# Rotating 96 images: 16 rows per partition and vector-engine block transposes in place of 4 rows per partition and matmul transposes

## The chip, the cores and the metric

The kernel runs on one core of one Trainium2 chip. The metric is device time in microseconds (us); lower is better. A "span" is the length of one profiled execution, from the first to the last instruction; the timed runs come out about 1.8 us above it.

Engine names: PE is the matmul engine, ACT the scalar engine, DVE the vector engine, SP the engine that here does nothing but issue transfers. The transfers themselves run on the core's 16 DMA engines, which the page counts together; SP issues all loads here and ACT all stores, so there are two DMA queues, q1 (loads) and q10 (stores).

## The reference

```python
x = np.random.randn(32, 3, 256, 256).astype(np.float32)

def reference(x):
    return np.rot90(x, k=1, axes=(-2, -1)).astype(np.float32)
```

These are 96 images of 256 x 256 floats, 25.17 MB in and 25.17 MB out. Each is rotated by a quarter turn: a transpose and a reversal of one axis. There is no arithmetic, so the least that any kernel must do is to move 50.33 MB between memory and the chip.

## The kernel before

A partition holds 4 rows of an image. Four rows of 256 floats are 4 KB that lie together in memory, so each transfer is made of runs of 4 KB. PE transposes 128 x 128 blocks into PSUM (the on-chip memory that PE writes here), ACT casts them to bf16, a second matmul puts the rows in the right order, and DVE copies the result to the output tile.

```python
    x_v4 = x.rearrange("b c (p d) w -> (b c) p d w", d=4)      # 4 rows per partition
    out_v4 = out.rearrange("b c (p d) w -> (b c) p d w", d=4)
    GROUPS = [8] * 11 + [4, 2, 2]                              # images per group
    # ... pools: 4 input tiles, 3 output tiles, 3 tail tiles, 2 + 2 PSUM tiles ...
    for gi, G in enumerate(GROUPS):
        S4 = in_pool.tile([P, G2, 4, W], fp32, tag="S", name="S4")
        nc.sync.dma_start(
            out=S4[:],
            in_=x_v4[i0 : i0 + G].rearrange("(j q) p d w -> (q p) j d w", q=2),
        )
        # ... U4: output tile ...
        for j in range(G2):
            for d4 in range(4):
                for par in range(2):
                    nc.tensor.transpose(...)                   # PE, 8 per image pair
            for q in range(2):
                nc.scalar.copy(out=bt[:], in_=p1pair[:, :, q, :])        # ACT, f32 to bf16
            for hh in range(2):
                for q in range(2):
                    nc.tensor.matmul(out=psum2[...], lhsT=exchh[hh][:], rhs=bts[q][:], ...)
            for hh in range(2):
                nc.vector.tensor_copy(out=U4[:, j, 2 * hh : 2 * hh + 2, :], in_=psum2[:, hh])
        nc.scalar.dma_start(                                   # the last three groups: after the loop
            out=out_v4[i0 : i0 + G].rearrange("(j q) p d w -> (q p) j d w", q=2),
            in_=U4[:],
        )
```

Of the kernel before, what the change touches and what calls it, by code (L numbers as in the profile page):

```python
# [1 line left out]

# [5 lines left out]


@with_exitstack
def kernel(
    ctx: ExitStack,
    tc: tile.TileContext,
    x: bass.AP,
    out: bass.AP,
):
    nc = tc.nc
    B, C, H, W = x.shape
    assert H == W == 256  # L20
    P = 128
    N = B * C

    x_v4 = x.rearrange("b c (p d) w -> (b c) p d w", d=4)
    out_v4 = out.rearrange("b c (p d) w -> (b c) p d w", d=4)

    GROUPS = [8] * 11 + [4, 2, 2]
    assert sum(GROUPS) == N
    assert all(g % 2 == 0 for g in GROUPS)

    fp32 = mybir.dt.float32
    bf16 = mybir.dt.bfloat16

    const_pool = ctx.enter_context(tc.tile_pool(name="const", bufs=1))
    in_pool = ctx.enter_context(tc.tile_pool(name="in_pool", bufs=4))
    bt_pool = ctx.enter_context(tc.tile_pool(name="bt_pool", bufs=4))
    out_pool = ctx.enter_context(tc.tile_pool(name="out_pool", bufs=3))
    tail_pool = ctx.enter_context(tc.tile_pool(name="tail", bufs=1))
    psum1_pool = ctx.enter_context(tc.tile_pool(name="psum1", bufs=2, space=bass.MemoryType.PSUM))
    psum2_pool = ctx.enter_context(tc.tile_pool(name="psum2", bufs=2, space=bass.MemoryType.PSUM))  # L40

    identity = const_pool.tile([P, P], fp32)
    make_identity(nc, identity)

    exchh = []
    for hh in range(2):
        e = const_pool.tile([P, P // 2], bf16, name=f"exch{hh}")
        nc.gpsimd.memset(e, 0.0)  # L48
        nc.gpsimd.affine_select(  # L49
            out=e,  # L50
            in_=e,
            compare_op=mybir.AluOpType.not_equal,
            fill=1.0,
            base=-(P - 1) + hh,
            pattern=[[2, P // 2]],
            channel_multiplier=1,
        )
        exchh.append(e)

    TAIL_N = 3  # L60
    deferred_stores = []

    i0 = 0
    for gi, G in enumerate(GROUPS):
        is_tail = gi >= len(GROUPS) - TAIL_N
        G2 = G // 2
        S4 = in_pool.tile([P, G2, 4, W], fp32, tag="S", name="S4")
        nc.sync.dma_start(
            out=S4[:],
            in_=x_v4[i0 : i0 + G].rearrange("(j q) p d w -> (q p) j d w", q=2),  # L70
        )
        S4_r = S4.rearrange("pp j d (k par) -> pp j d k par", par=2)

        if is_tail:
            U4 = tail_pool.tile(
                [P, G2, 4, W], fp32, tag=f"tail{gi}", name=f"U4_tail{gi}"
            )
        else:
            U4 = out_pool.tile([P, G2, 4, W], fp32, tag="U", name="U4")

        for j in range(G2):
            p1pair = psum1_pool.tile([P, 2, 2, W], fp32, name="p1pair")
            p1pair_r = p1pair.rearrange(
                "k dd q (pt dquad) -> k dd q pt dquad", dquad=4
            )
            for d4 in range(4):
                for par in range(2):
                    nc.tensor.transpose(  # L88
                        p1pair_r[:, 1 - par, :, :, d4],
                        S4_r[:, j, d4, :, par],  # L90
                        identity,
                    )
            bts = []
            for q in range(2):
                bt = bt_pool.tile([P, 2, W], bf16, name="bt")
                nc.scalar.copy(out=bt[:], in_=p1pair[:, :, q, :])  # L96
                bts.append(bt)

            psum2 = psum2_pool.tile([P, 2, 2, W], fp32, name="psum2")
            for hh in range(2):  # L100
                for q in range(2):
                    nc.tensor.matmul(  # L102
                        out=psum2[64 * q : 64 * q + 64, hh],
                        lhsT=exchh[hh][:],
                        rhs=bts[q][:],
                        start=True,
                        stop=True,
                    )

            for hh in range(2):  # L110
                nc.vector.tensor_copy(  # L111
                    out=U4[:, j, 2 * hh : 2 * hh + 2, :], in_=psum2[:, hh]
                )

        if is_tail:
            deferred_stores.append((i0, G, U4))
        else:
            nc.scalar.dma_start(
                out=out_v4[i0 : i0 + G].rearrange("(j q) p d w -> (q p) j d w", q=2),
                in_=U4[:],  # L120
            )
        i0 += G

    for s0, G, U4 in deferred_stores:
        nc.scalar.dma_start(  # L125
            out=out_v4[s0 : s0 + G].rearrange("(j q) p d w -> (q p) j d w", q=2),
            in_=U4[:],
        )


# [1 line left out]
_INS = ['x']  # L132
_OUTS = [((32, 3, 256, 256), 'float32')]


# [23 lines left out]
```

## Time and profile before

| | before |
|---|---|
| time when the prediction was made, median of 3 | 127.58 us (127.54 to 128.63) |
| profiled span | 125.8 us |
| busy: PE, DVE, ACT | 81%, 48%, 41% |
| transfer rate, 40 to 80 us | 420 GB/s |
| data packets | 12,288 of 4 KB (two queues of 6,144) |

The first lines are from the page of the kernel before. The first of them gives each engine's busy us, share of the span and number of instructions. The rows named DMA and GB/s divide the span into 40 equal slices: a 9 means that the 16 DMA engines were busy 90% of the slice or more, and GB/s is what they moved. The queue lines give packets, MB, and the time of those packets as a share of 16 engines' span. The last line is a group of like instructions: source line, engine, operation, output and input with their shapes, count, then busy us, mean ns of one, and the idle time before them with what ended most of it.

```profile
PE 101.3 (81%) x576; PEld 63.0 (50%) x576; DVE 60.5 (48%) x96; ACT 51.9 (41%) x97; POOL 1.2 (1%) x10
...
DMA  3999999999999999999999999999999999999993
GB/s 69 400 409 413 419 409 408 413 397 415 421 421 422 422 418 422 417 418 421 423 419 422 422 419 418 419 421 418 423 422 421 419 415 421 422 404 411 410 413 133
DMA packets 12742, 50.42 MB, mean 401 GB/s; under 512 B 448, under 2 KB 448, under 8 KB 12736
...
q1 hardware_dynamic: 6368, 25.17, 49.7%
q10 hardware_dynamic: 6368, 25.17, 48.9%
...
L111 DVE COPY U<-psum 128x512 f32<-128x512 f32 x88 | 55.5, 684 | 56.7 <-PE psum L102 44.7
```

The two queues together fill 98.6% of the DMA engines' time. DVE's copy of 128x512 floats takes 684 ns. The next view, windows, shows whether the rate follows PE. Its columns are: stretch, its length, busy time and number of instructions of PE, PEld, DVE, ACT and POOL, granted PE clock, DMA share, GB/s.

```profile
40.00:60.00 20.00, 19.67 (x115) 11.88 (x115) 12.24 (x21) 10.45 (x20) 0.00 (x0) 1.00 1.02 420
60.00:80.00 20.00, 16.20 (x99) 10.13 (x98) 9.78 (x17) 8.40 (x16) 0.00 (x0) 1.00 1.02 420
```

PE falls from 19.67 to 16.20 us of 20, and the rate stays at 420 GB/s. PE is busy, but it is not what bounds the kernel. The same is seen in the chain of waits (start, length, what), where the longest pieces are stores:

```profile
47.37 19.88 DMA out_dram<-U
...
73.94 23.12 DMA out_dram<-U
```

### The profile page before, as it was taken

To read this page: it belongs to the slowest core of one execution; us is meant where nothing else is said; L and a number is where in the kernel's file an instruction comes from. 1 tells how busy PE (TensorE), PEld (TensorE's weight loads), DVE (VectorE), ACT (ScalarE), POOL (GpSimd) and SP (SyncE) were. 2 spreads that over 40 slices of the span, in tenths; PEclk is the share of its full clock that TensorE was granted. 3 is DMA by queue.
4 is the path that set the end of the run, shared out by engine and by line. 5 is a ranking of instruction groups with operands and counts; after the bars stand their busy time and mean duration, and the time that the engine had idled before them with its cause. 6 is when DMAs were issued, how large, how long until landed. Compare 5 with 4: busy or idle time off the path is not lost.

```text
span 125.8 us, 1521 instructions
## 1 busy us (share of the span) xinstructions
PE 101.3 (81%) x576; PEld 63.0 (50%) x576; DVE 60.5 (48%) x96; ACT 51.9 (41%) x97; POOL 1.2 (1%) x10
## 2 busy tenths in 40 slices
PE   0029999999999999999995994897897699999500
PEld 0028556475576555655771761654654555755300
DVE  0000655565647744747445542842841945656520
ACT  4003363633653365336434435246246056336300
POOL 3000000000000000000000000000000000000000
PEclk9999999999999999999999999999999999999995
DMA  3999999999999999999999999999999999999993
GB/s 69 400 409 413 419 409 408 413 397 415 421 421 422 422 418 422 417 418 421 423 419 422 422 419 418 419 421 418 423 422 421 419 415 421 422 404 411 410 413 133
DMA packets 12742, 50.42 MB, mean 401 GB/s; under 512 B 448, under 2 KB 448, under 8 KB 12736
## 3 DMA queue, kind: packets, MB, share of 16 engines
q1 hardware_dynamic: 6368, 25.17, 49.7%
q10 hardware_dynamic: 6368, 25.17, 48.9%
q8 instruction: 4, 0.07, 0.2%
q14 instruction: 2, 0.02, 0.0%
HBM read 25.17 MB, written 25.17 MB: 400 GB/s over the span
## 4 chain that ended last, share of the span: by engine, by line
DMA 40%; PE 40%; DVE 7%; ACT 6%; issue 1%; DVEq 1%; ACTq 0%
DMA out_dram<-U 34%; PE p1pair L88 25%; PE psum L102 15%; DMA S<-in_x_dram 6%; ACT bt L96 6%; DVE U L111 4%; DVE U_tail L111 3%; DVEq L154 0%; ACTq L125 0%; DVEq L111 0%; ACTq L96 0%
## 5 line engine op out<-in xcount | busy, mean ns | idle before, releaser
L111 DVE COPY U<-psum 128x512 f32<-128x512 f32 x88 | 55.5, 684 | 56.7 <-PE psum L102 44.7
L96 ACT CAST bt<-p1pair 128x512 bf16<-128x512 f32 x96 | 50.6, 593 | 65.8 <-PE p1pair L88 65.8
L88 PE MATMUL p1pair<-identity,S 128*128 128x128 f32 x384 | 63.9, 305 | 8.8 <-DMA S<-in_x_dram 8.8
L88 PEld LDWEIGHTS p1pair<-identity,S 128*128 128x128 f32 x384 | 52.0, 209 | 30.2 <-issue 25.2
L102 PE MATMUL psum<-bt,exch 128*64 128x512 bf16 x192 | 45.0, 395 | 8.9 <-DVE U L111 7.0
L102 PEld LDWEIGHTS <-exch 128*64 128x64 bf16 x192 | 11.0, 107 | 25.4 <-DVE U L111 9.5
L111 DVE COPY U_tail<-psum 128x512 f32<-128x512 f32 x8 | 5.1, 685 | 3.1 <-PE psum L102 3.1
L96 ACT ACT_TABLE_LOAD x1 | 1.3, 1283 | 0.7 <-PEq L143 0.7
L49 POOL TENSOR_SCALAR_AFFINE_SELECT exch<-exch 128x64 bf16<-128x64 bf16 x2 | 0.4, 238 | 0.0
masks.py:199 POOL TENSOR_SCALAR_AFFINE_SELECT identity<-identity 128x128 f32<-128x128 f32 x1 | 0.3, 292 | 0.0
L48 POOL MEMSET exch<- 128x64 bf16 x2 | 0.2, 151 | 0.0
masks.py:197 POOL MEMSET identity<- 128x128 f32 x1 | 0.2, 204 | 0.3 <-POOLq L143 0.3
L143 POOL MEMSET const-bfloat16-1.0<- 128x1 bf16 x1 | 0.1, 101 | 0.0
L143 POOL MEMSET const-uint8-127<- 128x1 uint8 x1 | 0.1, 101 | 0.0
L143 POOL MEMSET const-float32-0.0<- 128x1 f32 x1 | 0.1, 98 | 0.2 <-issue 0.2
L143 POOL MEMSET const-float32-1.0<- 128x1 f32 x1 | 0.1, 98 | 0.0
## 6 DMA issues: line engine op xcount, KB each, us to landing
S<-in_x_dram SPq DMA_DIRECT2D x11, 2048.0 KB, 17.6
out_dram<-U ACTq DMA_DIRECT2D x11, 2048.0 KB, 18.4
S<-in_x_dram SPq DMA_DIRECT2D x1, 1024.0 KB, 16.8
S<-in_x_dram SPq DMA_DIRECT2D x2, 512.0 KB, 8.5
out_dram<-U_tail ACTq DMA_DIRECT2D x1, 1024.0 KB, 5.8
out_dram<-U_tail ACTq DMA_DIRECT2D x2, 512.0 KB, 5.1
```

The lines of the kernel that those rows point to most:

```text
L48: nc.gpsimd.memset(e, 0.0)
L49: nc.gpsimd.affine_select(out=e, in_=e, compare_op=mybir.AluOpType.not_equal, fill=1.0, base=-(P - 1) + hh, pattern=[[2, P // 2]], channel ...
L88: nc.tensor.transpose(p1pair_r[:, 1 - par, :, :, d4], S4_r[:, j, d4, :, par], identity,)
L96: nc.scalar.copy(out=bt[:], in_=p1pair[:, :, q, :])
L102: nc.tensor.matmul(out=psum2[64 * q : 64 * q + 64, hh], lhsT=exchh[hh][:], rhs=bts[q][:], start=True, stop=True,)
L111: nc.vector.tensor_copy(out=U4[:, j, 2 * hh : 2 * hh + 2, :], in_=psum2[:, hh])
L143: nc = _bacc.Bacc("TRN2", target_bir_lowering=False, num_devices=1)
```

## The change

Its intent is to make the runs longer on both sides. A partition now holds 16 rows of an image, 16 KB that lie together in memory, both for loads and for stores. An image then takes only 16 partitions. The kernel uses DVE's block transpose on blocks of 32 partitions by 32 elements (`A = 32 // K`), so two images share a block, and a second pair of images takes part on the free side: a group has 16 images (4 blocks of partitions, 2 images in each, 2 on the free side). PE, ACT's casts and PSUM are not used any more. The core of the diff:

```diff
-    x_v4 = x.rearrange("b c (p d) w -> (b c) p d w", d=4)
-    out_v4 = out.rearrange("b c (p d) w -> (b c) p d w", d=4)
-    GROUPS = [8] * 11 + [4, 2, 2]
+    R = 16
+    K = H // R          # 16 partitions per image
+    A = 32 // K         # 2 images per block of 32 partitions
+    G = 4 * A * A       # 16 images per group
+    F = R * W           # 4096 floats, 16 KB
+    x_v = x.rearrange("b c h w -> (b c h w)").rearrange(
+        "(g b a qk f) -> g b qk a f", b=A, a=A, qk=4 * K, f=F
+    )
+    o_v = out.rearrange("b c h w -> (b c h w)").rearrange(
+        "(g b a qk f) -> g a qk b f", b=A, a=A, qk=4 * K, f=F
+    )
     ... (PE transposes, casts, second matmul, copies, tail groups: removed) ...
+    in_pool = ctx.enter_context(tc.tile_pool(name="in_pool", bufs=3))
+    out_pool = ctx.enter_context(tc.tile_pool(name="out_pool", bufs=3))
+    for g in range(N // G):
+        S = in_pool.tile([P, A, F], fp32, name="S")
+        for b in range(A):
+            nc.sync.dma_start(out=S[:, b], in_=x_v[g, b])
+        U = out_pool.tile([P, A, F], fp32, name="U")
+        src = S.rearrange("p b (r k q) -> p q r k b", r=R, q=R)[:, ::-1, :, ::-1]
+        dst = U.rearrange("p a (q k r) -> p q r k a", q=R, r=R)
+        for q in range(R):
+            nc.vector.transpose(dst[:, q], src[:, q])
+        for a in range(A):
+            nc.scalar.dma_start(out=o_v[g, a], in_=U[:, a])
```

There are six groups with 16 transposes each. Neighbouring elements of a transpose's input and output are 64 bytes apart, or 16 KB when the step is from one image of a pair to the other.

More of the change, by code (lines that the diff above doesn't have):

```diff
@@ L5 @@
 import concourse.tile as tile
-from concourse import bass_utils, mybir
-from concourse.masks import make_identity
+from concourse import mybir
 from concourse._compat import with_exitstack
@@ L20 @@
     assert H == W == 256
+    N = B * C
     P = 128
-    N = B * C
-    x_v4 = x.rearrange("b c (p d) w -> (b c) p d w", d=4)
-    out_v4 = out.rearrange("b c (p d) w -> (b c) p d w", d=4)
-    GROUPS = [8] * 11 + [4, 2, 2]
-    assert sum(GROUPS) == N
-    assert all(g % 2 == 0 for g in GROUPS)
-    fp32 = mybir.dt.float32
-    bf16 = mybir.dt.bfloat16
-    const_pool = ctx.enter_context(tc.tile_pool(name="const", bufs=1))
-    in_pool = ctx.enter_context(tc.tile_pool(name="in_pool", bufs=4))
@@ L36 @@
-    bt_pool = ctx.enter_context(tc.tile_pool(name="bt_pool", bufs=4))
-    out_pool = ctx.enter_context(tc.tile_pool(name="out_pool", bufs=3))
-    tail_pool = ctx.enter_context(tc.tile_pool(name="tail", bufs=1))
-    psum1_pool = ctx.enter_context(tc.tile_pool(name="psum1", bufs=2, space=bass.MemoryType.PSUM))
-    psum2_pool = ctx.enter_context(tc.tile_pool(name="psum2", bufs=2, space=bass.MemoryType.PSUM))
-    identity = const_pool.tile([P, P], fp32)
-    make_identity(nc, identity)
-    exchh = []
@@ L46 @@
-    for hh in range(2):
-        e = const_pool.tile([P, P // 2], bf16, name=f"exch{hh}")
-        nc.gpsimd.memset(e, 0.0)
-        nc.gpsimd.affine_select(
-            out=e,
-            in_=e,
-            compare_op=mybir.AluOpType.not_equal,
-            fill=1.0,
-            base=-(P - 1) + hh,
-            pattern=[[2, P // 2]],
-            channel_multiplier=1,
-        )
-        exchh.append(e)
-    TAIL_N = 3
-    deferred_stores = []
-    i0 = 0
-    for gi, G in enumerate(GROUPS):
-        is_tail = gi >= len(GROUPS) - TAIL_N
-        G2 = G // 2
-        S4 = in_pool.tile([P, G2, 4, W], fp32, tag="S", name="S4")
-        nc.sync.dma_start(
-            out=S4[:],
-            in_=x_v4[i0 : i0 + G].rearrange("(j q) p d w -> (q p) j d w", q=2),
-        )
-        S4_r = S4.rearrange("pp j d (k par) -> pp j d k par", par=2)
-        if is_tail:
-            U4 = tail_pool.tile(
-                [P, G2, 4, W], fp32, tag=f"tail{gi}", name=f"U4_tail{gi}"
-            )
-        else:
-            U4 = out_pool.tile([P, G2, 4, W], fp32, tag="U", name="U4")
-        for j in range(G2):
-            p1pair = psum1_pool.tile([P, 2, 2, W], fp32, name="p1pair")
-            p1pair_r = p1pair.rearrange(
-                "k dd q (pt dquad) -> k dd q pt dquad", dquad=4
-            )
-            for d4 in range(4):
-                for par in range(2):
-                    nc.tensor.transpose(
-                        p1pair_r[:, 1 - par, :, :, d4],
-                        S4_r[:, j, d4, :, par],
-                        identity,
-                    )
-            bts = []
-            for q in range(2):
-                bt = bt_pool.tile([P, 2, W], bf16, name="bt")
-                nc.scalar.copy(out=bt[:], in_=p1pair[:, :, q, :])
-                bts.append(bt)
-            psum2 = psum2_pool.tile([P, 2, 2, W], fp32, name="psum2")
-            for hh in range(2):
-                for q in range(2):
-                    nc.tensor.matmul(
-                        out=psum2[64 * q : 64 * q + 64, hh],
-                        lhsT=exchh[hh][:],
-                        rhs=bts[q][:],
-                        start=True,
-                        stop=True,
-                    )
-            for hh in range(2):
-                nc.vector.tensor_copy(
-                    out=U4[:, j, 2 * hh : 2 * hh + 2, :], in_=psum2[:, hh]
-                )
-        if is_tail:
-            deferred_stores.append((i0, G, U4))
-        else:
-            nc.scalar.dma_start(
-                out=out_v4[i0 : i0 + G].rearrange("(j q) p d w -> (q p) j d w", q=2),
-                in_=U4[:],
-            )
-        i0 += G
@@ L124 @@
-    for s0, G, U4 in deferred_stores:
-        nc.scalar.dma_start(
-            out=out_v4[s0 : s0 + G].rearrange("(j q) p d w -> (q p) j d w", q=2),
-            in_=U4[:],
-        )
+    R = 16
[3 more added lines that the diff above has]
+    F = R * W
+    fp32 = mybir.dt.float32
+    x_v = x.rearrange("b c h w -> (b c h w)").rearrange(
[4 more added lines that the diff above has]
+    )
```

## The prediction

> **What bounds the kernel now.** The DMA engines. The page's DMA row is at 9 in 38 of 40 slices, and the two hardware queues take 49.7% and 48.9% of 16 engines' span. PE looks busy (81%), but the windows from 30 to 110 us show 420 GB/s whether PE is busy 98% or 83% of a stretch. The chain of waits names PE for 40% because buffers come free through it; its largest pieces are stores of 19.9 and 23.1 us that DVE waits for. About 2.6 us at the start and 2.1 us at the end of the 125.8 us span move almost nothing; the 121 us between run at 416 GB/s: 400 to 414 with loads alone (until 22 us), 420 mixed, 410 with stores alone. The measured 127.58 is 1.8 us above the profiled span.
>
> **What the change does.** It removes PE (101 us busy), ACT's casts (51 us) and 96 DVE copies of 684 ns (60 us), and adds 96 DVE block transposes of 128x512 f32. Bytes stay the same, so nothing removed lies on the critical path. What can move the time:
>
> 1. *Runs of 16 KB instead of 4 KB.* Each 4 KB packet occupied its engine for 157 ns (49.7% of 16 x 125.8 us over 6368 packets), 26.1 GB/s. [...]about 118 us for the data instead of 121: a gain of 2 to 3.5 us. If the hardware cuts at 4 KB the gain is nearly nil.
> 2. *Coarser pipeline.* First stores need 4 MB loaded plus 16 transposes: about 24 us (before: 21.9). Meanwhile three input buffers (12 MB, 30 us of DMA) keep the engines loaded. At the end the last 4 MB must be transposed before they are stored; the previous group's store covers that.
> 3. *DVE.* [...]a transpose takes about 0.68 us (estimate: as the 128x512 copy, 681 ns), 11 us per group of 16 images against 20 us of DMA (8.4 MB at 420 GB/s), 65 us in all: hidden. By my arithmetic DVE stays hidden up to about 1.0 us each. But each element is 64 bytes or 16 KB from the next, on both sides[...]. [...]No trace here shows a strided DVE access. I give that 22%.
>
> **Prediction.** 124.3 us: 4.7 us of ends, 118 us of data, 1.8 us from profile to timing. Range, lopsided for the DVE risk: 121.5 to 139. Faster by over 2% 0.50, within 2% 0.28, slower by over 2% 0.22.
>
> **What would show it.** Step 1: near 3,200 packets instead of 12,742, mixed windows at 425 or more. Step 2: DMA row at 9 in all inner slices, first store near 24 us. Step 3: transposes of 0.65 to 0.75 us, DVE busy near 65 us, waiting mostly for loads or free buffers. If wrong: transposes of 1.1 us or more, DVE busy 85% or more, and a tail in which DVE works while DMA is idle.
>
> **What would make it wrong.** The strided DVE rate; packets cut at 4 KB; memory-side conflicts of the 16 KB runs; a gap between last load and last store.

The sum was put down as 124.3 us; its three terms (4.7, 118 and 1.8) make 124.5. The 118 us of data (427 GB/s over 50.33 MB) stands as the author's estimate, not shown by a trace. In point 3 the 22% and the upper end of the range stand for a kernel bound by DVE, at about 142 us (e6 measured such a case at 140.33).

## The result, and the profile after

| | before | after |
|---|---|---|
| time, median of 4 runs each | 128.06 us (127.54 to 128.63) | 124.50 us (124.27 to 124.52) |
| ratio, 95% interval | | 0.972 (0.968 to 0.976) |
| profiled span | 125.8 us | 122.7 us |
| transfer rate, 40 to 60 us | 420 GB/s | 431 GB/s |
| time of one data packet, median | 159 ns (4 KB) | 611 ns (16 KB) |
| DVE busy | 60.5 us | 90.7 us |

A ratio is the mean time of one kernel's runs over that of the other's runs of the same rounds, so it is not quite the ratio of the medians that are quoted. The change is faster by 2.8%. The outputs are right.

The lines of the page after that answer to those of before:

```profile
DVE 90.7 (74%) x96; POOL 0.2 (0%) x4
...
DVE  0000699999999999999999999999906999930000
...
DMA  3999999999999999999999999999999999999992
GB/s 85 406 433 443 427 427 427 427 427 427 310 432 432 433 433 427 427 433 432 419 433 438 427 427 427 432 438 432 432 427 438 438 427 433 433 427 427 427 432 101
DMA packets 3457, 50.34 MB, mean 410 GB/s; under 512 B 384, under 2 KB 384, under 8 KB 384
...
q1 hardware_dynamic: 1728, 25.17, 48.9%
q10 hardware_dynamic: 1728, 25.17, 47.9%
...
L49 DVE STREAM_TRANSPOSE U<-S 128x512 f32<-128x512 f32 x96 | 90.7, 1055 | 17.7 <-DMA S<-in_x_dram 13.3
```

There are 3,072 data packets of 16 KB in place of 12,288 of 4 KB (the rest, 384 packets under 512 B and one more, is not data). The DMA row is full as before: the same engines are as busy, and each slice moves more. In the windows (the columns are now stretch, length, DVE, POOL, clock, DMA share, GB/s) the rate is 431 and 432 where it was 420:

```profile
40.00:60.00 20.00, 20.00 (x22) 0.00 (x0) 1.00 1.01 431
60.00:80.00 20.00, 19.82 (x22) 0.00 (x0) 1.00 1.01 432
```

Two things are not as expected. A transpose takes 1.06 us by its record, and 0.95 us from one start to the next (90.7 us over 96), not about 0.68. And the GB/s row has one slice at 310, near 32 us, that the kernel before does not have; it is called the dip below. The DMA row stays at 9 there: a packet that takes longer counts as busy too (25 load packets between 30 and 34 us take over 700 ns in place of 611), so a full DMA row is not yet a full rate.

### The profile page after: what moved, and what is told of

Read it like the earlier page. It is cut to its first block, busy times and chain, and to the rows that moved or that the text cites. A ratio compares the mean times of both kernels' runs of the same rounds, so it can differ in the third digit from the quotient of the medians.

```text
span 122.7 us, 182 instructions
## 1 busy us (share of the span) xinstructions
DVE 90.7 (74%) x96; POOL 0.2 (0%) x4
## 2 busy tenths in 40 slices
DMA packets 3457, 50.34 MB, mean 410 GB/s; under 512 B 384, under 2 KB 384, under 8 KB 384
## 4 chain that ended last, share of the span: by engine, by line
DMA 53%; DVE 31%; SPq 1%; issue 1%; DVEq 1%; ACTq 0%
DVE U L49 31%; DMA out_dram<-U 28%; DMA S<-in_x_dram 26%; SPq L43 1%; DVEq L77 1%; ACTq L51 0%; DVEq L49 0%
## 5 line engine op out<-in xcount | busy, mean ns | idle before, releaser
L49 DVE STREAM_TRANSPOSE U<-S 128x512 f32<-128x512 f32 x96 | 90.7, 1055 | 17.7 <-DMA S<-in_x_dram 13.3
```

What stands on the lines that cost most here:

```text
L49: nc.vector.transpose(dst[:, q], src[:, q])
```

## The experiments

Theory 1 is that the gain is the longer packet alone: a packet has a fixed time that does not grow with its size, and four times fewer packets pay it. The rival, theory 2, is that the gain comes from the rest: PE, ACT and PSUM emptied, fewer and larger tiles, a simpler pipeline.

### e1: the changed kernel again, beside e2 to e4 on the same chip

> Control on this chip: the changed kernel unedited. Both theories: 124.3 to 124.7 us, span 122.5 to 122.9, ratio to before 0.972, 16 KB packets of about 611 ns, transposes of 1.05 us, and the dip to about 310 GB/s in the slice near 32 us if it belongs to the kernel and not to one execution.

Measured: 124.78 us (124.35 to 124.88), just above the expected range, ratio 0.974 (0.970 to 0.979), before 127.93 us (127.50 to 128.35) on this chip. The dip is there again, at 288 GB/s in the same slice, so it belongs to the kernel:

```profile
GB/s 85 368 432 442 442 432 432 426 432 426 288 410 426 432 426 432 432 432 448 418 432 442 437 426 426 432 426 432 432 426 432 432 426 432 432 442 426 432 442 107
```

### e2: the kernel before with 16 KB runs

```diff
-            out=S4[:],
-            in_=x_v4[i0 : i0 + G].rearrange("(j q) p d w -> (q p) j d w", q=2),
+            out=S4.rearrange("p j d w -> p (j d w)"),
+            in_=flat(x_f, i0, G),     # the group's images as one stretch, cut in 128 equal runs
     ... the stores alike; all compute unchanged; the result is wrong on purpose ...
```

> The kernel before with nothing changed but the transfers' addresses: 16 KB runs in place of 4 KB (wrong result on purpose); PE, ACT and DVE work and all buffers stay. Theory 1 (packet size): about 3,600 packets of 611 ns, mixed windows at 430 GB/s, span 122.3 to 123.3, time 124.5 to 125.2. Theory 2 (the gain comes from the work taken off PE and ACT or from the larger tiles): time stays at 127.5 to 128.5 although packets are larger.

Measured: 125.27 us (125.22 to 125.45), ratio 0.979 (0.976 to 0.983), span 123.7 us: time and span are just above what theory 1 expected. By the 2% rule the verdict is "unclear", but the interval lies well under 1. The rate with PE at 19.64 of 20 us (columns as in the windows of before):

```profile
40.00:60.00 20.00, 19.64 (x115) 11.92 (x115) 12.24 (x20) 10.46 (x20) 0.00 (x0) 1.00 1.01 431
```

What follows: the addresses of the transfers alone, with all of the old compute in place, bring 2.66 us (127.93 less 125.27). The expected packet count was 3,600 and the page has 4,039 in all, because the small last groups keep runs of 8 KB and 4 KB. That is of use, since one run then holds three sizes: the median packet took 159 ns for 4 KB, 309 ns for 8 KB and 611 ns for 16 KB. From 4 to 16 KB that is 452 ns for 12,288 bytes, 27.2 GB/s per engine, and what is left of each packet is about 8 ns (159 less 4,096 bytes at 27.2 GB/s). The records of packets overlap a little, though: the DMA share is 1.02 with 4 KB and 1.01 with 16 KB. Worked out from the rates instead, 16 engines at 420 and 431 GB/s spend 156.0 ns on 4 KB and 608.2 ns on 16 KB, which leaves about 5 ns fixed (an estimate, and the one that counts for the time).

### e3: the changed kernel with 4 KB runs

```diff
-            nc.sync.dma_start(out=S[:, b], in_=x_v[g, b])
+            nc.sync.dma_start(
+                out=S[:, b].rearrange("p (c e) -> p c e", c=4)[:, ::-1], in_=runs(x, g * A + b)
+            )   # runs: the 2 MB in memory order, four pieces of 4 KB per partition, walked backwards
     ... the stores alike; the result is wrong on purpose ...
```

> The changed kernel with its transfers in 4 KB runs (wrong result on purpose: the pieces are walked backwards so that they are not joined); transposes and buffers stay. Theory 1 (packet size): about 12,300 packets of 159 ns, mixed windows at 420, span 125 to 126.5, time 127 to 128.3. Theory 2 (removed work, larger tiles): time stays at 124.3 to 125.

Measured: 127.21 us (127.16 to 127.28), ratio 0.994 (0.991 to 0.998), span 125.5 us.

```profile
DMA packets 12673, 50.34 MB, mean 401 GB/s; under 512 B 384, under 2 KB 384, under 8 KB 12672
...
40.00:60.00 20.00, 20.00 (x22) 0.00 (x0) 1.00 1.02 420
```

In the window from 40 to 60 us (columns as in the windows of after) the rate is 420 GB/s. What follows: with short packets the changed kernel keeps 0.7 us of its gain of 3.15 us (127.93 less 124.78 on this chip) and loses 2.43. Theory 2 expected it to keep all. The edit also changes the order in which memory is walked, but e2 and e3 agree from both sides: 4 KB runs gave 420 GB/s in two orders (before, e3), 16 KB runs 431 in two (the changed kernel, e2). The length of the runs is the cause of the bulk of the gain; 0.5 to 0.7 us belong to the rest of the change and were not divided further (the interval of e3, 0.991 to 0.998, allows 0.3 to 1.2 us).

The fixed time per packet is not the whole of it. From 10 to 30 us, before any store, loads run alone; first e3, then the changed kernel:

```profile
10.00:20.00 10.00, 5.61 (x6) 0.00 (x0) 1.00 1.03 411
20.00:30.00 10.00, 10.00 (x12) 0.00 (x0) 1.00 1.02 408
...
10.00:20.00 10.00, 6.67 (x8) 0.00 (x0) 1.00 1.00 428
20.00:30.00 10.00, 10.00 (x12) 0.00 (x0) 1.00 1.02 437
```

There the longer runs gain over 5%, twice the 2.6% of the mixed windows, and 5 ns per packet do not explain that; no run shows why. The dip takes most of it back: counted from the packets, e1 has moved 12 MB at 31.2 us and e3 at 32.6, but 13 MB at 34.7 and 35.0.

### e4: transposes of neighbouring elements

```diff
-        src = S.rearrange("p b (r k q) -> p q r k b", r=R, q=R)[:, ::-1, :, ::-1]
-        dst = U.rearrange("p a (q k r) -> p q r k a", q=R, r=R)
+        src = S.rearrange("p b f -> p (b f)").rearrange("p (q e) -> p q e", q=R)   # wrong result
+        dst = U.rearrange("p a f -> p (a f)").rearrange("p (q e) -> p q e", q=R)   # on purpose
```

> The changed kernel with each block transpose on 512 neighbouring elements on both sides (wrong result on purpose), transfers as in the changed kernel. Theory 1: DVE is hidden, so time stays within 0.5 us of 124.5 whatever a transpose takes. Rival: DVE at 74% busy is part of the time, and a shorter transpose gains over 1 us. For the transpose itself, theory S (steps of 64 bytes and 16 KB slow it): about 0.65 us each in place of 1.05, DVE busy near 62 us. Theory W (a 4-byte block transpose has this rate anyhow): 1.05 us unchanged.

Measured: 124.50 us (124.48 to 124.61), ratio 0.973 (0.970 to 0.976).

```profile
L50 DVE STREAM_TRANSPOSE U<-S 128x512 f32<-128x512 f32 x96 | 58.4, 675 | 54.6 <-DMA S<-in_x_dram 44.7
```

What follows: DVE falls from 90.7 to 58.4 us busy, waits 54.6 us, and the time does not move against e1 (124.78). DVE is hidden. The step between elements is what makes the kernel's transposes long: 0.61 us from start to start with neighbours (58.4 over 96), 0.95 us with the kernel's steps.

### e5: which steps cost

```diff
         for q in range(R):
-            nc.vector.transpose(dst[:, q], src[:, q])
     ... (six branches in its place; group 0, L57: as it was; 1, L59: neighbours on both sides;
     2, L61: 64-byte steps in the input alone; 3, L63: in the output alone; 4, L65: 8-byte steps
     on both sides; 5, L67: 16-byte steps on both sides; the result is wrong on purpose) ...
```

> One look at the transpose alone: the six groups of the changed kernel use six pairs of steps, one source line each (wrong result on purpose). e4 gave 0.67 us with neighbouring elements on both sides against 1.06 us. Theory S1 (each side adds its share): in-only and out-only between 0.8 and 0.9 us. Theory S2 (the slower side sets the rate): one of them 1.06, the other 0.67. Steps of 8 bytes on both sides: near 0.67[...]; steps of 16 bytes on both sides: as slow as 64 bytes[...].

The timeline of DVE (start, length of the 16 together, line, what, count, the wait before):

```profile
13.35 15.21 DVE L57 STREAM_TRANSPOSE U<-S 128x512 f32<-128x512 f32 x16 [13.35 <-DMA S<-in_x_dram]
28.41 9.59 DVE L59 STREAM_TRANSPOSE U<-S 128x512 f32<-128x512 f32 x16
...
37.90 14.77 DVE L61 STREAM_TRANSPOSE U<-S 128x512 f32<-128x512 f32 x16
54.28 13.91 DVE L63 STREAM_TRANSPOSE U<-S 128x512 f32<-128x512 f32 x16 [1.61 <-DMA out_dram<-U]
73.83 9.61 DVE L65 STREAM_TRANSPOSE U<-S 128x512 f32<-128x512 f32 x16 [5.64 <-DMA out_dram<-U]
93.16 15.42 DVE L67 STREAM_TRANSPOSE U<-S 128x512 f32<-128x512 f32 x16 [9.72 <-DMA out_dram<-U]
```

Per transpose that is 0.95 us as it was, 0.60 with neighbours, 0.92 with steps in the input alone, 0.87 in the output alone, 0.60 with 8-byte steps and 0.96 with 16-byte steps (by the records, which the expectation was put in: 1.06, 0.69, 1.01, 1.00, 0.67 and 1.07). Neither S1 nor S2 holds as it was put: either side alone costs nearly the whole of it (0.27 to 0.32 of 0.35 us), and both together hardly more than one. Steps of 8 bytes on both sides are free here (0.60 us, as with neighbours); steps of 16 bytes, and of 64 bytes and more, on both sides cost a factor of 1.6 (0.96 and 0.95 us). The runs do not show why.

### e6: 20 transposes per group

```diff
-        for q in range(R):
+        for q in [*range(R), *range(4)]:     # four done twice; the result stays right
```

> The changed kernel with 4 of the 16 transposes of each group done twice (result stays right): 20 starts of 0.95 us, 19 us per group[...]. Theory 1 (DVE hidden only up to about 1.0 us per transpose): DVE busy without a pause from 13 to 128 us, then two last stores of about 5 us each that nothing covers: span near 140, time near 142, DMA row with gaps. Rival (buffers of three groups on each side take it up): under 130.

Measured: 140.33 us (140.32 to 140.36), ratio 1.096 (1.088 to 1.104), span 138.6 us. DVE has no pause any more and the DMA row has gaps:

```profile
DVE  0001999999999999999999999999999999994000
POOL 0000000000000000000000000000000000000000
DMA  3999999995999999999999999999980799103895
```

What follows: with 18.8 us of DVE per group (112.7 us over 6) the kernel is bound by DVE, and the two last stores are covered by nothing, as theory 1 had it. The expectation of 142 was 1.7 us high.

### e7: the first store with 4 KB runs

```diff
-            nc.scalar.dma_start(out=o_v[g, a], in_=U[:, a])
+            n = 4 if g == 0 and a == 0 else 1
+            for c in range(n):
+                e = slice(c * F // n, (c + 1) * F // n)
+                nc.scalar.dma_start(out=o_v[g, a][:, :, e], in_=U[:, a, e])
```

> The changed kernel with its first store alone cut in four transfers with 4 KB runs (result stays right). e1 and e4 both lose about 1 us of transfer where the first store sets in, and e3 with 4 KB runs does not. Theory D1 (the dip comes from 16 KB packets of the two queues meeting for the first time): no slice under 400 GB/s, span about 0.8 us shorter, time 123.6 to 124.0. Theory D2 (it comes from the load queue's large packets, whatever is stored): dip stays near 300 GB/s, time as e1, 124.4 to 124.8.

Measured: 124.33 us (124.17 to 124.41), ratio 0.971 (0.965 to 0.977), against 124.53 for e8 on the same chip. The expected 123.6 to 124.0 was missed. The run is not the clean test that it was meant to be: a quarter of the store needs only four transposes, so the first store was issued at 17.3 us, not at 28.6, and the dip moved to the slices from 18.4 to 24.5 us, which are at 368 and 409 GB/s. It is smaller and not gone. The cut also moved the later transfers: a new slice of 348 GB/s near 112 us, just after the last stores are issued, may hide part of what the time could have shown.

### e8: one load on the store queue

```diff
-            nc.sync.dma_start(out=S[:, b], in_=x_v[g, b])
+            queue = nc.scalar if g == 0 and b == 1 else nc.sync
+            queue.dma_start(out=S[:, b], in_=x_v[g, b])
```

> The changed kernel with the second load of group 0 issued by ACT's queue (result stays right), so that this queue has been used once before the first store. Theory D3 (the dip is the store queue's first use): no dip near 30 us, perhaps one near 3 us, and the first store's data start 1.4 us after its issue in place of 4.8; time 123.6 to 124.0. Rival (the dip comes with the first writes to memory): dip stays, time within 0.3 of e1.

Measured: 124.53 us (124.34 to 124.56), ratio 0.972 (0.967 to 0.978). The two slices from 30.7 to 36.8 us are at 331 and 347 GB/s: the dip stays, and the first store's data still start 5.0 us after its issue (30.42 to 35.40 us). D3 falls: it is not the first use of the queue.

### e9 and e10: long packets on one side only

Both start from e3; e9 takes the stores from the changed kernel, e10 the loads.

```diff
 # e9, against the changed kernel (e10 has this on the stores instead)
-            nc.sync.dma_start(out=S[:, b], in_=x_v[g, b])
+            nc.sync.dma_start(
+                out=S[:, b].rearrange("p (c e) -> p c e", c=4)[:, ::-1], in_=runs(x, g * A + b)
+            )
```

> The changed kernel with 4 KB runs on loads alone (wrong result on purpose). Theory 1 (a fixed time per packet, the same in both directions): half of the gain of e1 over e3, span 123.8 to 124.6, time 125.6 to 126.2. Dip: if it needs large packets on the load queue, no slice under 390 GB/s after 10 us; if large store packets make it, one slice near 300 as in e1.

> The changed kernel with 4 KB runs on stores alone (wrong result on purpose). Theory 1: half of the gain, span 123.8 to 124.6, time 125.6 to 126.2. Dip: if it needs large packets on the load queue, one slice near 300 GB/s when the first store sets in; if large store packets make it, none under 390. Both e9 and e10 without it: both queues must have large packets.

Measured: e9 134.46 us (134.07 to 134.54), ratio 1.052 (1.048 to 1.055); e10 128.32 us (128.16 to 128.38), ratio 1.004 (1.001 to 1.007). Both expectations of time, 125.6 to 126.2, were wrong by far, e9 by over 8 us. The rate row of each kernel, first e9:

```profile
GB/s 49 384 423 409 407 412 410 409 409 412 451 420 433 409 443 412 443 447 384 455 404 425 428 412 410 432 434 464 405 393 421 448 435 370 5 0 158 474 395 237
```

```profile
GB/s 83 414 414 430 445 445 420 414 435 435 347 435 427 421 400 436 434 435 414 435 427 429 421 408 416 420 422 423 418 423 422 418 423 420 417 159 271 409 410 236
```

Until 30 us and in the middle the rates are near what was expected. Near the end e9 has a hole in which almost nothing moves, and e10 a shallower one (159 and 271 GB/s). They follow from how the two queues shared the DMA engines in these runs. Counted from the trace's packets, in GB/s of loads and of stores over 5 us:

| stretch | changed kernel | e3, 4 KB both | e9, loads 4 KB, stores 16 KB | e10, loads 16 KB, stores 4 KB |
|---|---|---|---|---|
| 50 to 55 us | 216 and 223 | 211 and 210 | 100 and 357 | 341 and 96 |
| 70 to 75 us | 220 and 213 | 211 and 211 | 81 and 347 | 338 and 88 |

With equal packets the queues got about equal shares (211 and 211 GB/s in e3, from 70 to 75 us); with packets of 4 to 1 they got about 4 to 1 (347 and 81 in e9). Counted in packets, that is about the same number from each queue: in e9, from 70 to 75 us, about 20 load packets and 21 store packets per us. So a queue's share went with its packet size. In e9 the loads starve: the last load ends at 103.9 us, against 91.8 in the changed kernel, and the last transposes and stores follow with nothing left to overlap. In e10 the stores starve, the loads are through at 76.4 us, and DVE waits for output tiles:

```profile
DVE U L56 <- DMA out_dram<-U: 4.9, 1, 4.9
DVE U L56 <- issue: 4.6, 1, 4.6
```

The second wait has no named releaser; it ends at 83.4 us, about 0.5 us after the last packet of the fourth store (82.8 us), whose tile these transposes write.

As for the dip: e10 has it (347 GB/s near 32 us), e9 has not. With e3, which has none, it goes with large packets on the load queue while the first store sets in; with 4 KB stores it is there too, if anything shallower (e10, e7). D2 is the theory that fits best. It does not need the new transposes: e2, with all of the old compute, has it as well (339 GB/s from 24.7 to 27.8 us). Nor is it a lack of loads: in e4, where it is at 288 GB/s, about 16 load packets are in flight all the time from 16 to 18 us. In the changed kernel, 25 load packets that start between 30 and 34 us take over 700 ns in place of 611, the longest 1,796. Why they do is open. The dip of e1 is worth about 1.0 us of transfer ((431 less 288) over 431, times a slice of 3.07 us).

### e11 and e12: 17 and 18 transposes per group

```diff
-        for q in range(R):
+        for q in [*range(R), *range(1)]:     # e11; range(2) in e12; the result stays right
```

> 17 transposes per group (one done twice, result right). e6 had 0.94 us per start, 13.4 us before the first and 12.5 us of span after the last. Theory 1: 13.4 + 102 x 0.94 + 12.5 = 121.8 us is still under the DMA's 122.8, so span 122.5 to 123.5, time 124.3 to 125.2.

> 18 transposes per group (two done twice, result right). Theory 1: 13.4 + 108 x 0.94 + 12.5 = 127.4 us is over the DMA's 122.8, so DVE sets the span: 126.8 to 128, time 128.5 to 129.8, slower than the kernel before. Rival (buffers take it up): under 125.5.

Measured: e11 124.19 us (124.08 to 124.27), ratio 0.972 (0.969 to 0.975), span 122.5; e12 129.32 us (129.25 to 129.41), ratio 1.012 (1.010 to 1.015), span 127.6, against 127.4 expected. In e11 the only long wait of DVE is for the first load:

```profile
DVE U L49 <- DMA S<-in_x_dram: 13.5, 1, 13.5
```

The busy lines of the two pages, first e11:

```profile
DVE 96.1 (78%) x102; POOL 0.2 (0%) x4
...
DVE 101.7 (80%) x108; POOL 0.2 (0%) x4
```

So 17 transposes of 0.94 us, 16.0 us per group (96.1 over 6), are just hidden, and 16.9 us (101.7 over 6) cost 5 us and make the kernel 1.2% slower than the one before. The changed kernel, with 15.1 us per group (90.7 over 6), stands 6% under that edge.

No version that clearly beats both was found: e7 and e11 lie within 0.4 us of the changed kernel on other chips, with ratios whose intervals overlap its own.

## Why the prediction was right

The time (124.3 us predicted, 124.50 measured) and the direction were right. Point by point:

1. **What bounds the kernel: right.** e2 kept all the old PE, ACT and DVE work and gained 2.66 us from addresses alone.
2. **Longer packets: right, in cause and size.** The mixed windows went from 420 to 431 GB/s (predicted: 425 or more), and packets fell to 3,457 (predicted: near 3,200). The gain in span is 3.1 us (predicted: 2 to 3.5); e2 and e3 give 2.4 to 2.7 us of the gain to the longer runs. How the prediction came from longer packets to 118 us of data was the author's estimate and not shown; the rates measured since, 420 and 431 GB/s, leave about 5 ns fixed per packet (an estimate). The 5% of the stretch with loads alone was not foreseen. From the first to the last packet the data took 119.5 us, not 118, and the ends (2.1 us before the data start, 1.1 us after they end) 3.2 us, not 4.7. That is mostly where the line is drawn: drawn in the same way, the kernel before has 122.6 us of data and 3.2 us of ends, so the data gained 3.1 us, where the prediction had 3. There is luck in it all the same: 431 GB/s in place of the 427 that the 118 us come to is worth about 1.2 us over 50.33 MB (an estimate), and the dip, which nobody had predicted, took about 1 us back.
3. **Coarser pipeline: right that it costs nothing, wrong in its dates.** The DMA row is 9 in all inner slices. The first store was issued at 28.6 us and its data started at 33.4 us, not at 24, because the 16 transposes took 15 us and not 11. Loads filled the time, except for the dip.
4. **DVE: hidden, as predicted, but its term was mis-sized by 40%.** The term that failed reads "a transpose takes about 0.68 us". Measured: 0.95 us per transpose and 90.7 us in all, not 65. The record of a transpose of neighbours is 0.675 us (e4), so the estimate was right for a transpose without steps. The strided transpose lies between the two cases of the prediction: 1.06 us by its record, above the 0.65 to 0.75 us expected and under the "1.1 us or more" that would have shown it wrong. From start to start it is 0.95 us against 0.60 us with neighbours (e5).
5. **The edge at 1.0 us per transpose: right.** e11 (1.00 us per sixteenth of a group) costs nothing and e12 (1.06 us) costs 5 us. The DVE-bound time of 142 us, which e6 expected for 19 us per group, was measured as 140.3. The risk of 22% that the prediction gave to this was real: the kernel missed it by 6%.

## What to carry to other kernels

When the DMA engines are full and the bytes cannot shrink, make the contiguous run per partition longer: going from 4 to 16 KB was worth 2.6% of rate here, whatever the compute engines did. Make it longer on both sides at once, because unequal packets on the two queues split the engines about in proportion to their size here (347 and 81 GB/s with 16 and 4 KB in e9); a longer run on the stores alone made the kernel 5% slower than the one before, and on the loads alone it gained nothing (e10). Before giving an engine strided work in exchange, compute how much time per group stays hidden, and measure the strided instruction: here steps of 16 bytes or more on both sides cost a factor of 1.6 (0.95 and 0.96 us against 0.60) and 8 bytes nothing.

## Figures measured here

- Packets by size, of transfers that SP and ACT issue (e2): 159 ns for 4 KB, 309 for 8 KB, 611 for 16 KB, that is 27.2 GB/s per engine and a fixed part of about 8 ns by the records, which overlap a little, and of about 5 ns by the rates (an estimate). Loads alone gained over 5% from 4 to 16 KB (411 and 408 GB/s in e3, 428 and 437 in the changed kernel), more than either figure explains.
- Two queues with packets of 16 and 4 KB: the shares were 347 and 81 GB/s (e9), and the kernel lost 5%.
- DVE block transposes of 128x512 f32 (e5): 0.60 us with steps of 4 or 8 bytes, 0.96 us with 16, 0.95 us with 64 bytes and more on both sides, 0.92 and 0.87 us with 64 bytes on the input or the output alone. With neighbours (e4): 0.675 us by the record, 0.61 us from start to start.
- The dip: with 16 KB packets on the load queue, the rate fell to between 282 and 347 GB/s for one or two slices of about 3 us when the first store set in (the changed kernel, e1, e2, e4, e5, e8, e10, e11, e12), and not with 4 KB loads (e3, e9). In e6 the slice is at 137, but there the first input tile comes free only near the first store's issue at 32.4 us, and loads wait for it too (an estimate: e1 has its first 12 MB, three tiles, at 31.2 us); in e7 it is shallower (368 and 409). Its cause is open.
